# Stores issued from GpSimd's queue, loads alone on SyncE's, in a one-core decoder layer

## The chip, the cores and the metric

The kernel is one program on 1 core of a Trainium2 chip. The metric is the device time of one execution in microseconds (us); the median of several runs counts. The core's engines work from separate instruction streams: TensorE (PE, with its weight loads as PEld), VectorE (DVE), ScalarE (ACT), GpSimd (POOL) and SyncE (SP). SP computes nothing here; it issues the DMAs, and its stream is named SPq in the profile. An engine's stream runs in order: an instruction that waits for a semaphore holds up all that stands behind it.

## The reference

One layer of a decoder over 1024 tokens of width 1024, all float32. It runs a half-step SwiGLU feed-forward (hidden width 2816), one projection of the normalised rows into all branches' operands, three attentions (with forget bias, sparse over the 256 best keys of an indexer, and into 256 memory tokens), a gated merge, and a second half-step feed-forward:

```python
h = h + 0.5 * swiglu(rmsnorm(h, ffn1_norm[l]), ffn1_w_gate[l], ffn1_w_up[l], ffn1_w_down[l])
u = rmsnorm(h, mix_norm[l])
(fq, fk, fv, ff, dq, dk, dv, iq, ik, iw, mq, g) = jnp.split(u @ w_in[l], SPLIT_POINTS, axis=-1)
...
o_a = fox_attention(fq, fk, fv, logf)
o_b = dsa_attention(dq, dk, dv, iq, ik, iw, k_sel)
o_c = memory_attention(mq, km, vm)
...
proj = jnp.einsum('bsnw,nwd->bsnd', branches, w_branch[l])
gates = jax.nn.sigmoid(g.reshape(B, S, N_BRANCHES, D))
h = h + jnp.sum(gates * proj, axis=2) @ w_out[l]
h = h + 0.5 * swiglu(rmsnorm(h, ffn2_norm[l]), ffn2_w_gate[l], ffn2_w_up[l], ffn2_w_down[l])
```

## The kernel before

Every matrix product is made of three products of numbers split into a high and a low part, so each weight tile that arrives (`wS`) is cast by ACT (`wH`) and the rest is taken by DVE (`wL`, line 230's `split`). Two slots of `wS`, or four while a second pool is open, hold arriving weights; the next load into a slot can go out when DVE has finished with it.

The stages follow one another on PE:

- Memory keys and values and the first normalisation (0 to about 70 us in the trace), then feed-forward 1 to about 708 us. Its hidden rows go to a scratch tensor in HBM (`hid_s`, 44 stores of 512 KB out of `gu` tiles, which have three buffers) and come back for the second half.
- The projection, about 715 to 1138 us. It is made in blocks of 512 columns: `mq` (memory queries), `iq` (indexer queries), `fk`, `fq`, `fv` (forgetting attention), `dq` (sparse queries). A block takes its 128-row units one by one: 24 matmuls into `tm`, then a norm on ACT and DVE, a transpose on PE and a split into `th` and `tl` (`turn`, line 801). Each half is stored to the block's scratch tensor as 128 partitions of 4 runs of 128 numbers (128x4x128, runs of 512 bytes). `th` and `tl` have two buffers each, so unit n+2 may write its `th` only when the store of unit n's has landed. `fox_values` (line 1533) splits values into an `iqs` tile of 128x8x128, with two buffers too. Units of the indexer load their stored queries back (`iqs<-iq_s`, line 1472) and score keys (`isc`).
- The heads, about 1138 to 1550 us: queries, keys, values and masks are loaded back; outputs go to `o_s` and the sums' reciprocals to `r_s`. The gate projection fills gaps on PE from 715 us on (`gate`, 48 stores of `sg`, two buffers, to `g_s`).
- The merge to about 1803 us (`branch`, line 1183): gates come back as `bg` (three buffers), partial sums go to `mg_s` and come back as `bm`; the tile `bg` is what is stored to `mg_s`.
- The output projection and norm to about 1915 us, with 8 stores of `h` to `h_s`; then feed-forward 2, whose last step adds into `rows` and stores 8 row tiles to `out`.

The order in which the work is written comes from a planner (`_Flow`) with costs of PE, ACT and DVE; it knows nothing of queues. A scheduler of the language then lists the instructions of every engine, with a model of each DMA's duration in which the queue counts, so a change of queue can swap neighbours on all engines.

All DMAs go through two helpers, `load` (line 172) and `store` (line 175). In the kernel before both use SP's queue, so SP's stream holds 326 stores between its loads. POOL's stream holds the constants at the start and 32 small memsets for the rotary tables (line 844). The program is built with this line, 1705, which sets aside room for the descriptors of DMAs that GpSimd issues:

```python
nc = bacc.Bacc("TRN2", target_bir_lowering=False, num_devices=1, dynamic_dma_scratch_size=1024)
```

Of the kernel before, what the change touches and what calls it, by code (L numbers as in the profile page):

```python
# [155 lines left out]
def trunk_layer_kernel(  # L156
# [5 lines left out]
    nc = tc.nc  # L162
# [6 lines left out]
    def plain(ap):  # L169
        return ap.bitcast(F32) if ap.dtype == F32R else ap  # L170
# [2 lines left out]
        nc.sync.dma_start(plain(o), plain(i))  # L173

    def store(o, i):
        nc.sync.dma_start(plain(o), plain(i))

    class Pool:

# [50 lines left out]
    def split(high, low, v):  # L230
        A.copy(high, v)
        V.tensor_sub(low, v, high.bitcast(F32))
# [194 lines left out]
    class FeedForward:  # L427
# [57 lines left out]
        def job(self, j):  # L485
# [41 lines left out]
            if not gate:  # L527
                for i in range(2):
                    store(hid_s[j // 2 + i * HF], u[:, 2 * i:2 * i + 2].rearrange("p a t -> p (a t)"))
# [233 lines left out]
    def scratch(name, shape):  # L763
        return dram.tile(shape, F32, name=name)
# [8 lines left out]
    fv_s = scratch("fv_s", [8, P, NT, P])  # L773
# [41 lines left out]
    def store_pairs(dst, t, parts):  # L815
        for i, th in enumerate(parts):
            store(dst[i].rearrange("(a b) d t -> (b d) a t", b=2)[:, :, t * P:(t + 1) * P], th)


    def mem_keys(tp):  # L820
        def consume(t, pt):
            xn = head_norm(tp, pt, 4, 2)
            yield
            for i, v in enumerate(turn(tp, xn)):
                store(km_s[:, :, i].rearrange("h p m -> p h m")[:, :, t * P:(t + 1) * P], v)
        return consume
# [706 lines left out]
    def fox_values(t, pt):  # L1533
        vt = tp.tile([P, 8, P], F32R, tag="iqs", name="iqs", bufs=2)
        split(vt[:, :, 0:64], vt[:, :, 64:128], pt.rearrange("p (h d) -> p h d", h=8))
        store(fv_s.rearrange("h p t d -> p h t d")[:, :, t], vt)
        return
        yield

    blocks = [(mq_block, normed(mq_s, 4, gmx[:, 0:1])), (mk_block(C_IQ), index_queries),  # L1540
              (mk_block(C_FK), normed(fk_s, 8, None)), (mk_block(C_FQ), normed(fq_s, 8, gfx[:, 0:1])),
              (mk_block(C_FV), fox_values), (mk_block(C_DQ), sparse_queries)]
    chains = block_chains(blocks, uh, ul, NT)
    fl.run(chains[:2] + [prep] + chains[2:], width=5, filler=gates_f, background=sel_c, margin=0.5)
# [100 lines left out]
    h = [h2[:, t] for t in range(NT)]  # L1645
# [70 lines left out]
```

## Time and profile before

| | us |
|---|---|
| median of 3 runs (2552.12 to 2558.94) | 2553.32 |
| the profiled execution, its own time | 2555.42 |
| span of its trace, first to last instruction | 2553.4 |
| PE busy in the span | 2426.6 (95%) |
| DVE busy | 1641.0 (64%) |
| ACT busy | 1146.6 (45%) |
| POOL busy | 2.2 |

PE's mean granted clock is 0.978 of full speed. One DMA queue carries 349.62 MB in 297744 packets. An engine's idle time costs something only where the chain of waits that ends last runs through it, so the views to read are the busy time by stage, the waits by engine, and the chain. Time outside the span (2555.42 - 2553.4 = 2.0 us) is taken as fixed.

### The profile page before, as it was taken

The numbers are of one execution on the slowest core, as the hardware profiler recorded it, in microseconds if no ns is written. First come the engines' busy times: TensorE is split into PE (matmuls) and PEld (weight loads), VectorE is DVE, ScalarE is ACT, GpSimd is POOL, SyncE is SP. The second block draws the span as 40 slices with busy tenths as digits, with TensorE's granted clock in tenths as the row PEclk, the third lists the DMA queues.
The fourth block names the chain that finished last, engine by engine and source line by source line (L and its number), as shares of the span: only waits on it lengthen the run. The fifth ranks groups of instructions, "written<-read, shape, count | busy, mean of one in ns | idle before, by whom it ended". The sixth has DMA issues, their size and how long they took to land.

```text
span 2553.4 us, 31738 instructions
## 1 busy us (share of the span) xinstructions
PE 2426.6 (95%) x11532; PEld 2007.0 (79%) x11532; DVE 1641.0 (64%) x3405; ACT 1146.6 (45%) x1904; POOL 2.2 (0%) x40
## 2 busy tenths in 40 slices
PE   6999999999999999989999998999979999999998
PEld 4788888888777878767777886877768888888887
DVE  7855555488757578685667556777376554554885
ACT  5533333333433366657886555543144333333332
POOL 0000000000000000000000000000000000000000
PEclk9899999999999999998999999999989999999999
DMA  7222222474334534544455535756422222225743
GB/s 232 75 80 78 91 84 79 158 302 137 127 123 144 158 106 133 157 141 147 122 156 141 146 108 177 235 173 226 169 85 66 91 66 91 91 71 191 271 151 129
DMA packets 297900, 351.64 MB, mean 138 GB/s; under 512 B 18792, under 2 KB 199688, under 8 KB 297744
## 3 DMA queue, kind: packets, MB, share of 16 engines
q1 hardware_dynamic: 297744, 349.62, 42.8%
q8 instruction: 90, 1.47, 0.2%
q14 instruction: 66, 0.54, 0.1%
HBM read 254.98 MB, written 93.54 MB: 136 GB/s over the span
## 4 chain that ended last, share of the span: by engine, by line
PE 72%; DVE 12%; ACT 7%; DMA 5%; issue 4%; SPq 0%; ACTq 0%; DVEq 0%
PE gx L51 19%; PE gy L51 14%; PE tm L51 8%; PE dx L51 8%; PE dy L51 7%; PE gate L51 6%; ACT junk L51 3%; PE br L51 3%; DVE wL L51 2%; PE po L51 2%; PE pT L51 2%; PE sp L51 2%; DMA wS<-in_w_in 1%; DMA bg<-g_s 1%; ACT ns L51 1%
## 5 line engine op out<-in xcount | busy, mean ns | idle before, releaser
L51 ACT CAST wH<-wS 128x1024 fp32r<-128x1024 f32 x238 | 225.5, 953 | 303.1 <-PE gy L51 102.8
L51 PE MATMUL gx<-th,wH 128*128 128x512 f32 x880 | 318.3, 394 | 7.2 <-ACT th L51 7.2
L51 DVE TENSOR_TENSOR wL<-wS,wH 128x1024 fp32r<-128x1024 f32 x238 | 260.3, 1099 | 88.4 <-ACT wH L51 87.7
L51 PE MATMUL gx<-th,wL 128*128 128x512 f32 x704 | 275.5, 391 | 0.0
L51 PE MATMUL tm<-wH,uh 128*128 128x512 f32 x496 | 200.5, 405 | 9.2 <-ACT wH L51 5.6
L51 PE MATMUL gy<-th,wH 128*128 128x512 f32 x528 | 206.3, 391 | 1.2 <-ACT th L51 1.2
L51 PE MATMUL gx<-tl,wH 128*128 128x512 f32 x528 | 205.4, 389 | 0.0
L51 PE MATMUL gy<-th,wL 128*128 128x512 f32 x528 | 205.4, 389 | 0.0
L51 PE MATMUL gy<-tl,wH 128*128 128x512 f32 x528 | 205.4, 389 | 0.0
L51 ACT ACTIVATE junk<-wk,sn 128x384 bf16<-128x384 f32 (+5 forms) x186 | 164.3, 883 | 89.4 <-DVE sn L51 77.2
L51 PEld LDWEIGHTS gx<-th,wH 128*128 128x128 f32 x880 | 167.5, 191 | 43.1 <-ACT th L51 8.0
L51 PE MATMUL tm<-wL,uh 128*128 128x512 f32 x496 | 197.0, 397 | 1.8 <-DVE wL L51 1.0
L51 PE MATMUL tm<-wH,ul 128*128 128x512 f32 x496 | 196.6, 396 | 0.0
L51 ACT CAST wH<-S 128x1024 fp32r<-128x1024 f32 x88 | 92.3, 1051 | 170.3 <-PE gy L51 167.0
L51 DVE TENSOR_TENSOR wL<-S,wH 128x1024 fp32r<-128x1024 f32 x88 | 107.5, 1223 | 87.8 <-ACT wH L51 87.8
L51 DVE TENSOR_TENSOR gu<-gu,gy 128x512 f32<-128x512 f32 x88 | 60.3, 685 | 157.3 <-PE gy L51 81.6
L51 PE MATMUL gate<-uh,wH 128*128 128x512 f32 x384 | 157.5, 410 | 0.0
L51 DVE TENSOR_TENSOR pl<-pT,ph 128x512 fp32r<-128x512 f32 (+1 forms) x176 | 109.8, 637 | 73.6 <-ACT ph L51 72.9
L51 PEld LDWEIGHTS gx<-th,wL 128*128 128x128 f32 x704 | 133.3, 189 | 27.8
L51 PE MATMUL gate<-uh,wL 128*128 128x512 f32 x384 | 153.4, 400 | 0.0
L51 PE MATMUL gate<-ul,wH 128*128 128x512 f32 x384 | 153.0, 398 | 0.0
L51 PE MATMUL dx<-wH 128*128 128x512 f32 x352 | 137.5, 391 | 2.2 <-DVE rows L51 2.1
(265 smaller groups left out, 5196.9 us busy)
## 6 DMA issues: line engine op xcount, KB each, us to landing
wS<-in_ffn_w_down SPq DMA_DIRECT2D x70, 512.0 KB
wS<-in_w_in SPq DMA_DIRECT2D x48, 512.0 KB
wS<-in_ffn_w_gate SPq DMA_DIRECT2D x44, 512.0 KB
wS<-in_ffn_w_up SPq DMA_DIRECT2D x44, 512.0 KB
hid_s<-gu SPq DMA_DIRECT2D x44, 512.0 KB
a<-hid_s SPq DMA_DIRECT2D x30, 512.0 KB
g_s<-sg SPq DMA_DIRECT2D x48, 256.0 KB
bg<-g_s SPq DMA_DIRECT2D x48, 256.0 KB
```

Source lines behind the costliest of these rows:

```text
L51: return fn(*a, **k)
```

## The change

`store` issues on GpSimd's queue, `load` stays on SP's. With that, POOL's stream holds all stores, in an order of its own, and SP's holds loads alone. `fox_values` stores its tile in two halves of four heads, so 8 stores become 16 and there are 334 in all.

```diff
     def store(o, i):
-        nc.sync.dma_start(plain(o), plain(i))
+        nc.gpsimd.dma_start(plain(o), plain(i))
...
     def fox_values(t, pt):
         vt = tp.tile([P, 8, P], F32R, tag="iqs", name="iqs", bufs=2)
         split(vt[:, :, 0:64], vt[:, :, 64:128], pt.rearrange("p (h d) -> p h d", h=8))
-        store(fv_s.rearrange("h p t d -> p h t d")[:, :, t], vt)
+        for i in (0, 4):
+            store(fv_s[i:i + 4].rearrange("h p t d -> p h t d")[:, :, t], vt[:, i:i + 4])
```

The order of PE's matmuls stays the same but for small swaps (the gate products stand between the same units of the projection). The DMAs' order is shown at three places. First, SP's stream before, at the end of the `fq` block and the start of `fv` in the projection (`wk` is a load of indexer scores, `mk` the mask made from them):

```order
L176 DMA fq_s<-tl 128x4x128
L173 DMA wS<-in_w_in 128x2x512 x2
L176 DMA fq_s<-th 128x4x128
L176 DMA fq_s<-tl 128x4x128
L173 DMA wS<-in_w_in 128x2x512 x2
L176 DMA fv_s<-iqs 128x8x128
L176 DMA fq_s<-th 128x4x128
L176 DMA fv_s<-iqs 128x8x128
L176 DMA fq_s<-tl 128x4x128
L173 DMA wk<-sc_s 128x896
L176 DMA fv_s<-iqs 128x8x128
L176 DMA mask_s<-mk 128x512
```

Now POOL's stream after the change, at the same place:

```order
L176 DMA sc_s<-acc 128x1024
L176 DMA fq_s<-th 128x4x128
L176 DMA fq_s<-tl 128x4x128
L176 DMA fq_s<-th 128x4x128
L176 DMA fq_s<-tl 128x4x128
L176 DMA fv_s<-iqs 128x4x128 x2
L176 DMA fq_s<-th 128x4x128
L176 DMA fv_s<-iqs 128x4x128 x2
L176 DMA fq_s<-tl 128x4x128
L176 DMA mask_s<-mk 128x512
L176 DMA fv_s<-iqs 128x4x128 x12
L176 DMA dq_s<-th 128x4x128
```

The weight loads no longer stand between the stores, and the fv stores have become sixteen of the size of the others. From the first `fq` store to the last `fv` store POOL's stream holds 32 of these, one `sc_s` and one `mask_s`.

Second, SP's stream before at the end of `dq`, where the loads of the first memory head follow:

```order
L176 DMA dq_s<-tl 128x4x128
L176 DMA g_s<-sg 128x512
L176 DMA dq_s<-th 128x4x128
L176 DMA dq_s<-tl 128x4x128
L173 DMA wS<-in_w_in 128x8x128
L173 DMA qs<-mq_s 128x1024
L173 DMA vs<-mq_s 128x1024
L173 DMA km<-km_s 128x512
```

And SP's stream after, at those loads:

```order
L173 DMA wS<-in_w_in 128x8x128 x3
L173 DMA wk<-sc_s 128x1024
L173 DMA wS<-in_w_in 128x8x128
L173 DMA qs<-mq_s 128x1024
L173 DMA vs<-mq_s 128x1024
L173 DMA km<-km_s 128x512
```

The loads of queries and keys have kept the weight load ahead of them and lost the stores.

Third, SP's stream before in the merge, where a row of reciprocal sums (`rs`) is stored and read back (`oR`):

```order
L173 DMA bm<-mg_s 128x512
L176 DMA o_s<-os 64x512
L173 DMA bg<-g_s 128x512
L176 DMA r_s<-rs 8x128
L176 DMA mg_s<-bg 128x512
```

And POOL's stream after, towards the end of the merge:

```order
L176 DMA mg_s<-bg 128x512 x3
L176 DMA o_s<-os 64x512
L176 DMA r_s<-rs 8x128
L176 DMA mg_s<-bg 128x512
```

The store of `rs` stands behind other stores only; the load into `bg` ahead of it is gone from its stream.

## Rows read from the trace of the kernel before

**Rows 1.** The page's part 1: busy time and share of the span.
```profile
PE 2426.6 (95%) x11532; PEld 2007.0 (79%) x11532; DVE 1641.0 (64%) x3405; ACT 1146.6 (45%) x1904; POOL 2.2 (0%) x40
```

**Rows 2.** Windows: stretch, its us; busy us by engine; PE clock, DMA share, GB/s.
```profile
128.00:700.00 572.00, 570.26 (x2517) 471.47 (x2516) 349.65 (x438) 206.12 (x263) 0.00 (x0) 1.00 0.38 127
...
777.00:1138.00 361.00, 347.08 (x1581) 281.96 (x1581) 269.63 (x933) 189.44 (x373) 0.00 (x0) 0.98 0.46 132
...
1550.00:1803.00 253.00, 229.35 (x1219) 191.68 (x1218) 189.97 (x367) 114.00 (x214) 0.00 (x0) 0.97 0.67 216
...
1920.00:2490.00 570.00, 569.89 (x2514) 471.66 (x2513) 342.34 (x402) 205.96 (x262) 0.00 (x0) 1.00 0.36 122
```

**Rows 3.** Waits of SP's queue: waiter <- releaser: us in total, times, longest.
```profile
SPq L173 <- DVE wL L51: 715.9, 156, 32.4
SPq L176 <- DVE gu L51: 219.2, 44, 9.6
SPq L176 <- ACT th L51: 177.1, 39, 14.1
```

**Rows 4.** Waits of ACT and PE for loads.
```profile
ACT wH L51 <- DMA wS<-in_w_in: 23.1, 15, 4.5
...
PE spm L51 <- DMA km<-km_s: 6.8, 2, 4.6
```

**Rows 5.** Tile views of five scratch tensors: stores; issue ns min/median/max, first to last start.
```profile
L176 SPq DMA_DIRECT2D mq_s<-th x8: 359/360/367, 777.4 to 823.2; - x8
...
L176 SPq DMA_DIRECT2D fk_s<-th x8: 359/360/385, 905.4 to 968.9; - x8
...
L176 SPq DMA_DIRECT2D fq_s<-th x8: 359/360/422, 978.6 to 1034.6; - x8
...
L176 SPq DMA_DIRECT2D fv_s<-iqs x8: 359/360/499, 1029.4 to 1071.9; - x8
...
L176 SPq DMA_DIRECT2D dq_s<-th x8: 359/360/370, 1093.5 to 1136.5; - x8
```

**Rows 6.** Timeline of SP in the iq block: start us, us, engine, line, op, out<-in.
```profile
849.18 0.37 SPq L176 DMA_DIRECT2D iq_s<-th  x1
850.78 0.36 SPq L176 DMA_DIRECT2D iq_s<-tl  x1
851.36 2.19 SPq L173 DMA_DIRECT2D iqs<-iq_s  x2
```

**Rows 7.** The chain that ended last, in the merge: start us, us, what.
```profile
1702.58 3.42 DMA mg_s<-bg
...
1710.19 2.90 DMA r_s<-rs
```

**Rows 8.** Timeline of SP at the end of the dq block.
```profile
1137.33 0.36 SPq L176 DMA_DIRECT2D dq_s<-tl  x1
1137.74 0.55 SPq L173 DMA_DIRECT2D wS<-in_w_in  x1
```

**Rows 9.** Timeline of DVE at three places; in brackets idle time before, and releaser.
```profile
1135.48 1.23 DVE L51 TENSOR_TENSOR wL<-wS,wH 128x1024 fp32r<-128x1024 f32 x1
...
1706.82 0.27 DVE L51 COPY rs<-rT 8x128 f32<-8x128 f32 x1
...
1866.44 1.28 DVE L51 SCALAR_TENSOR_TENSOR h<-h,rs_y,gain_row 128x1024 f32<-128x1024 f32 x1 [1.62 <-DMA h_s<-h]
```

**Rows 10.** Timeline of DVE at the end.
```profile
2545.36 2.73 DVE L51 SCALAR_TENSOR_TENSOR rows<-dx,rows 128x512 f32<-128x512 f32 x4 [4.40 <-PE dx L51]
```

**Rows 11.** Timeline of SP at the end.
```profile
2546.08 2.81 SPq L176 DMA_DIRECT2D out<-rows  x4
```

**Rows 12.** The page's part 5: busy us, mean ns of one | idle before, releaser.
```profile
L51 DVE TENSOR_TENSOR wL<-wS,wH 128x1024 fp32r<-128x1024 f32 x238 | 260.3, 1099 | 88.4 <-ACT wH L51 87.7
```

**Rows 13.** Tile view of inv_freq: the rotary memsets and their reader.
```profile
L844 POOL MEMSET inv_freq<- x32: 98/98/100, 744.7 to 745.7; 128x1 f32 x32
L51 DVE TENSOR_TENSOR angles<-pos_f,inv_freq x1: 426/426/426, 754.9 to 754.9; 128x256 f32<-128x256 f32 x1
```

## The prediction

> **What bounds the kernel now.** I read the page's busy times first. PE is busy 95% of the span [rows 1], so at most 126.8 us (2553.4 - 2426.6) can be won, and any stall of PE is paid in full. Next the windows by stage [rows 2]: both feed-forwards run with PE busy throughout (570.26 of 572 us, 569.89 of 570). PE's idle time that DMAs could touch lies in the projection (361.0 - 347.1 = 13.9 us) and the merge (23.7 us). Then the waits [rows 3]: the longest in total on SP's queue are of loads for DVE to free a weight slot (715.9 us), after that come stores that wait for what they store (219.2 us for `gu`, 177.1 for `th`). While SP stands in one of the latter, the loads behind it stand too. That is what the change takes away. What it could pay is seen on the other side [rows 4]: ACT waited 23.1 us for weights of the projection, PE itself 6.8 us for `km`.
>
> **What is moved.** All 334 stores go to POOL, which has 2.2 us of work [rows 1]. No trace here shows a store on POOL, so its service is bounded from the nearest rows. Two prices matter: how soon POOL can issue the next one, and how long one takes to land.
>
> Landing, as it is: the store of `iq_s<-th` is issued at 849.18 and the load that reads it goes out at 851.36 [rows 6], so a 256 KB store of 128x4x128 lands in at most 2.2 us from SP. From POOL I bound it by 2.2 and by twice that, 4.4 (making the descriptors in software costs as much as the whole trip), and take 3.4: the chain has the trip of a 256 KB store beside other traffic at 3.42 us [rows 7], and the projection has traffic beside its stores at a DMA share of 0.46 [rows 2].
>
> Issue: SP takes 0.36 us for one [rows 5]. For POOL the ends are 0.36 (no dearer) and 3.4 (nothing overlaps). For stores with long rows I take 1.0, the middle of the two as a ratio. For the 128x4x128 stores I take the upper end: one must have landed before the next is issued. The reason is in the kernel: it sets aside 1024 bytes for such descriptors, and the edit halves the `fv` store, whose size is double theirs; if double does not fit, two of them at once hardly do.
>
> [...]
>
> **The bursts of the projection.** The stall arises through the buffers: unit n+2 writes `th` on ACT only when unit n's store has landed. Behind ACT's waiting split stand the next unit's square, the relu of index scores and the weight casts, and PE waits for all of them. So before a block's last unit, all its stores but the last four must have gone (for `fv` the last four halves). With 3.4 us a piece:
> - `mq`: 12 stores need 40.8 us; the units' first stores span 823.2 - 777.4 = 45.8, less 0.8 for the split ahead of the store: 45.0. No stall.
> - `fk`: 12 and 4 others at 1.0 need 44.8, in 63.5. None. The `iq` block has six units in about the time of eight; none.
> - `fq` and `fv` together: 16 + 12 = 28 and 2 others need 97.2 us; 978.6 to 1071.9, less 1.3 for both splits, gives 92.0. Stall 5.2.
> - `dq`: 12 and 2 others need 42.8, in 1136.5 - 1093.5 - 0.8 = 42.2. Stall 0.6.
>
> Together +5.8 us [rows 5].
>
> **Landings that are waited for.** Each is 3.4 - 2.2 = 1.2 us later. On the chain I count six: two of `mg_s` (3.42 us and one like it) and one of `r_s` (2.90) in the merge [rows 7], the `iq_s` reload at the first score [rows 6], the `h_s` store that DVE awaited for 1.62 us before it normalises in place [rows 9], and the last `out` store. 6 x 1.2 = +7.2.
>
> **The end.** DVE finishes four row tiles from 2545.36 on in 2.73 us [rows 10], the first at about 2546.05. SP issues them by 2546.08 + 2.81 = 2548.9 [rows 11]. POOL needs 4 x 1.0 from 2546.1: 2550.1. +1.2.
>
> **What is won.** Where a load stood behind a store without another reason. At 1137.33 SP issues the last `dq` store and at 1137.74 the weight load ahead of the memory heads' queries [rows 8]; DVE had freed a slot at 1135.48 + 1.23 = 1136.71 [rows 9]. So 1.0 of the 6.8 us before `km`. In the merge `rs` is ready at 1707.09 [rows 9] and its store is issued at 1710.19 [rows 7], behind a load into `bg`: 3.1 us. Together -4.1.
>
> **What costs nothing.** The 44 `hid_s` stores: PE is full there and `gu` has three buffers, so a job's store has longer than a job (570 us for 22 pairs, 26 us a pair) to land; the cover goes only if a store takes some 20 us. The 48 `g_s` stores: two `sg` buffers, and one is filled every 9 us (412 us of heads for fewer than 48). The rotary memsets now stand behind two `g_s` stores; they ended at 745.7 and are read at 754.9 [rows 13], so they can be 9 us late.
>
> **The sum.** 5.8 + 7.2 + 1.2 - 4.1 = +10.1 on the profiled execution's 2555.4 (2.1 above the median of 2553.3): 2565.5, which is 2563 as a median.
>
> **Rivals.**
> [...]
> - No difference: a store takes 2.9 or less. Then 28 x 2.9 + 2 = 83.2 fits in 92.0 and no burst stalls; 6 x 0.7 + 1.2 - 4.1 = +1.3, 2555. For it: 2.2 from SP, and the likely surcharge is unknown.
> - Faster: landing again 2.9 or less, and free loads pay more than the two places I found. All 6.8 us before `km`, a third of ACT's 23.1 (7.7, the rest being idle time off the path) and the 3.1 of `rs` go: 5.4 - 17.6 = -12.2, 2541. It decides where weight loads went out late because of a store by 4.5 us or more, the longest such wait. Against: 156 loads waited for DVE's slot, which stays.
>
> **How the numbers follow.** My forecast has 0.40, its own range 2556 (3.1 us a store: no burst, 5.4 + 1.2 - 4.1) to 2577 (3.7: 13.6 + 4.2 in bursts, 9.0 + 1.2 - 4.1). The slow rival has 0.20, no difference 0.27, faster 0.13. Within 0.3% is 2545.7 to 2561.0, about what a measurement here can tell from no change. Same: 0.27 and 0.04 of the forecast's lower part, 0.31. Faster: 0.13, and 0.01 of the second rival's edge. Slower: 0.55. The range for eight in ten goes from 2546, leaving out most of the fast rival, to 2620, leaving out the slow rival's upper half.
>
> **What would show it.** Right: POOL issuing 128x4x128 stores no closer than about 3.4 us while it has a backlog; ACT's `th` and `iqs` splits waiting for stores in `fv` and `dq`, by some 6 us; feed-forwards unchanged in length; `rs` stored within a microsecond. Wrong: these stores issued a microsecond apart (two at once do fit), or spaced 4.5 us and more; the projection as long as before or tens of us longer; waits of ACT for weights gone.

## The result and the profile after

The changed kernel takes 2580.06 us (median of 4 runs, 2573.85 to 2582.76), the one before beside it 2552.79. The ratio is 1.0098, 95% interval 1.0074 to 1.0122: slower by 25 us, between 19 and 31. The profiled execution took 2573.85 us, the shortest of the four; its span is 2572.1, which is 18.7 more than before.

First the rows that answer to [rows 1] and [rows 2]. Part 1 of the page of after:

```profile
PE 2429.3 (94%) x11532; PEld 2009.4 (78%) x11532; DVE 1645.8 (64%) x3405; ACT 1145.7 (45%) x1904; POOL 204.8 (8%) x374
```

PE does the same work, and POOL now has 204.8 us of it for 334 stores. The windows of after (columns as in [rows 2]). The second and the third are the projection from its first `mq` store on and the merge; they start and end at the same matmuls as those of [rows 2]. The first and the last lie in the feed-forwards:

```profile
128.00:700.00 572.00, 570.77 (x2520) 472.01 (x2519) 351.31 (x438) 205.45 (x263) 12.80 (x24) 1.00 0.38 127
779.60:1160.80 381.20, 351.78 (x1581) 283.79 (x1580) 272.90 (x945) 194.28 (x382) 83.20 (x119) 0.96 0.36 123
1568.50:1824.80 256.30, 233.57 (x1220) 195.47 (x1218) 190.28 (x367) 113.77 (x214) 29.06 (x54) 0.95 0.65 209
1940.00:2510.00 570.00, 569.90 (x2515) 471.88 (x2514) 343.98 (x403) 205.04 (x262) 13.87 (x26) 1.00 0.37 123
```

The feed-forwards are as full as before. The projection's stretch is 20.2 us longer (381.2, 361.0 before) with the same 1581 matmuls in it. PE is idle there for 381.2 - 351.8 = 29.4 us, where it was 13.9; the other 4.7 us are the matmuls themselves, at a mean granted clock of 0.96 where it was 0.98. The merge is 3.3 us longer, none of it idle time of PE.

What SP waits for in after, beside [rows 3]:

```profile
SPq L173 <- DVE wL L51: 1099.7, 164, 30.1
SPq L173 <- DMA mg_s<-bg: 86.0, 27, 6.1
```

No store stands ahead of a load on SP's stream any more. Its loads wait longer instead: for DVE's weight slots (1099.7 us, 715.9 before), as one expects when SP comes to the same wait sooner, and for stores to `mg_s` to land (86.0 us, 33.7 before). The waits for loads that [rows 4] shows, in after:

```profile
ACT wH L51 <- DMA wS<-in_w_in: 26.5, 13, 6.8
...
PE spm L51 <- DMA km<-km_s: 8.6, 2, 6.4
```

Both have grown. So at these two places the freed loads paid nothing.

Where the time went is read by taking the same matmul (by its tile names and count) in two traces, and subtracting its start in before. This is worked out from the traces, in us:

| matmul at, in before | after | room 1408 | + old order | + h_s on SP |
|---|---|---|---|---|
| 690, feed-forward 1 | -1.1 | -3.2 | +0.4 | -3.3 |
| 734, start of the projection | +2.9 | +0.5 | +5.3 | -3.4 |
| 815, end of mq | +2.8 | +0.6 | +4.9 | -5.0 |
| 868, iq block | +7.4 | +0.9 | +4.7 | -3.2 |
| 954, fk block | +11.1 | +4.4 | +5.7 | -1.4 |
| 1040, fv block | +16.6 | +10.8 | +7.0 | +0.3 |
| 1120, dq block | +21.9 | +11.5 | +6.4 | -0.2 |
| 1300, heads | +18.8 | +9.3 | +7.3 | -0.3 |
| 1600, merge | +18.8 | +9.2 | +11.2 | -1.8 |
| 1640, merge | +24.5 | +15.8 | +11.9 | -0.1 |
| 1940, feed-forward 2 | +18.2 | +9.0 | +1.3 | -9.6 |

The last three columns are experiments below. A single trace is good for a step of several us at one place and not for a total: the runs of before alone lie between 2543 and 2559, and the last column ends at -9.6 though the median of its kernel equals before's. What all four win between 1640 and 1940 can't be told from chance by it.

### The profile page after: what moved, and what is told of

Same layout as the page of the kernel before. It is cut to its first block, busy times and chain, and to the rows that moved or that the text cites. A ratio compares the mean times of both kernels' runs of the same rounds, so it can differ in the third digit from the quotient of the medians.

```text
span 2572.1 us, 31970 instructions
## 1 busy us (share of the span) xinstructions
PE 2429.3 (94%) x11532; PEld 2009.4 (78%) x11532; DVE 1645.8 (64%) x3405; ACT 1145.7 (45%) x1904; POOL 204.8 (8%) x374
## 3 DMA queue, kind: packets, MB, share of 16 engines
q0 software_dynamic: 28640, 94.61, 10.0%
## 4 chain that ended last, share of the span: by engine, by line
PE 59%; issue 16%; DVE 12%; ACT 6%; DMA 5%; POOL 2%; SPq 0%; POOLq 0%; ACTq 0%; DVEq 0%
PE gx L51 19%; PE gy L51 14%; PE dy L51 6%; PE dx L51 6%; PE tm L51 6%; PE gate L51 3%; ACT junk L51 3%; DVE wL L51 2%; DMA wS<-in_w_in 1%; PE nar L51 1%; PE br L51 1%; ACT wH L51 1%; DVE rs_a L51 1%; DVE hsq L51 1%; ACT ns L51 1%
## 5 line engine op out<-in xcount | busy, mean ns | idle before, releaser
L51 DVE TENSOR_TENSOR S<-wS 128x512 f32<-128x512 f32 x88 | 57.3, 688 | 160.8 <-DMA wS<-in_ffn_w_gate 92.6
```

Source lines behind the costliest of these rows:

```text
L51: return fn(*a, **k)
```

## The experiments

The theories: A, the room for GpSimd's descriptors makes the 128x4x128 stores follow one another; B, a store costs more on a second queue whatever its size, since transfers compete and land later; C, GpSimd's own work on a store or DVE's work spaces the stores; and, added after the first runs, D, the scheduler's new order of the instructions costs time by itself. The first runs have `sp_store` beside `store`, which issues on SP as before; `store` issues on GpSimd.

**The blocks' stores back on SP.**

```diff
-            store(dst[i].rearrange("(a b) d t -> (b d) a t", b=2)[:, :, t * P:(t + 1) * P], th)
+            sp_store(dst[i].rearrange("(a b) d t -> (b d) a t", b=2)[:, :, t * P:(t + 1) * P], th)
...
-        for i in (0, 4):
-            store(fv_s[i:i + 4].rearrange("h p t d -> p h t d")[:, :, t], vt[:, i:i + 4])
+        sp_store(fv_s.rearrange("h p t d -> p h t d")[:, :, t], vt)
```

> The 128x4x128 stores of the projection (mq, iq, fk, fq, dq; fv unsplit) go back to SyncE; all other stores stay on GpSimd. Theory A (the room for GpSimd's descriptors holds one such store, and they are spaced 2.85 us and more, which holds up th, tl and iqs): the projection, 20 us longer in the trace after, is within 4 us of before; the start of the projection (+4), the merge (+4) and the heads (-5) stay as after; about 2556 to 2560. Theory B (any store on GpSimd's queue costs, since transfers on two queues compete and land later): the projection keeps 10 us or more, 2568 or more.

Measured: 2563.45 us, ratio 1.0037 (1.0023 to 1.0051). Some 16 us come back (1.0098 - 1.0037), so these stores carry the larger part; but 10 us stay, more than theory A allowed, and 6 of them arise between 976 and 1006 us, where this kernel has none of them on GpSimd's queue. Neither theory had that. In the traces TensorE, ScalarE and VectorE run their instructions, and SP its loads, in the same order here as in after, so the 16 us are a comparison with the order held, and the 6 us are for theory D to explain.

**Only the blocks' stores on GpSimd** (all other calls read `sp_store`).

> The reverse: only the 128x4x128 stores (fv in two halves) are issued by GpSimd, all other stores by SyncE. Theory A: the projection is 15 to 22 us longer than before and nothing else moves, 2568 to 2576. Theory B: under 8 us, 2555 to 2561.

Measured: 2564.21 us, ratio 1.0043 (1.0028 to 1.0058): 11 us, between the two forecasts. The block stores cost something without the others: `iq_s`, `fv_s` and `dq_s` stores stand in its chain. But its order of instructions is a third one, neither that of before nor that of after, so not all of the 11 us need be theirs; and the two halves (10 and 11) do not quite make the 25 to 27 of the whole.

**More room.**

```diff
-    nc = bacc.Bacc("TRN2", target_bir_lowering=False, num_devices=1, dynamic_dma_scratch_size=1024)
+    nc = bacc.Bacc("TRN2", target_bir_lowering=False, num_devices=1, dynamic_dma_scratch_size=1408)
```

> After, with dynamic_dma_scratch_size=1408 instead of 1024, nothing else. [...]

Measured: 2564.60 us, ratio 1.0044 (1.0030 to 1.0058): within the 2560 to 2570 that theory A had for two stores at a time, and below the 2575 to 2583 of theory C. The order of all instructions in its trace is that of after, so some 14 us (1.0098 - 1.0044) belong to the room alone. The timeline of POOL in after, in the fv block (columns as in [rows 9]):

```profile
1070.16 0.76 POOL L176 DMA_DIRECT2D fv_s<-iqs  x1 [1.55 <-issue]
1073.04 0.75 POOL L176 DMA_DIRECT2D fv_s<-iqs  x1 [2.12 <-issue]
1075.89 0.76 POOL L176 DMA_DIRECT2D fv_s<-iqs  x1 [2.10 <-issue]
```

and the same block with 1408:

```profile
1054.44 1.50 POOL L176 DMA_DIRECT2D fv_s<-iqs  x2 [2.01 <-DVE iqs L51]
1060.84 1.50 POOL L176 DMA_DIRECT2D fv_s<-iqs  x2 [4.90 <-DVE iqs L51]
```

In after a piece follows 2.85 us behind the last; with more room two go in 1.50 us, and POOL waits for DVE's split, which is the data. The chain of after tells what the 2.85 are:

```profile
1073.04 2.55 DMA fv_s<-iqs
```

This store lands at 1075.59, and the next starts at 1075.89, 0.30 us later. In the trace of after 79 stores of this size directly follow another one on POOL's stream. None starts earlier than 0.30 us behind the landing of the one ahead, and 69 start within 0.4 us of it; with 1408, 49 of the 79 start before the one ahead has landed. Theory C falls.

**The smallest room that should do.** The same edit with 1088.

> [...] If stores are admitted whole when their descriptors fit, this is as good as 1408: 2561 to 2568, spacing 0.75 us within a pair. If the room's effect grows with its size, hardly better than 1024: 2573 to 2582.

Measured: 2566.64 us, ratio 1.0053 (1.0040 to 1.0067), the stores again in pairs of 1.50 us. 64 bytes more give back 11 us; 320 more on top add little that can be told apart (the intervals overlap). With 1024 bytes, 94% of 1088, none of the 79 stores starts before the one ahead has landed, so in these runs a store is admitted whole or not at all.

**Only the stores to g_s, o_s and r_s on GpSimd.** The other calls read `sp_store`.

> Only the stores to g_s, o_s and r_s are issued by GpSimd; all others, the projection's among them, by SyncE. If the 5 us that the heads gained after (at 1238 to 1260 us of before) came from loads of queries and keys that stood behind such stores on SyncE's queue, this kernel has them without the loss: 2545 to 2550. If they were a part of earlier delays that was made up, nothing: 2552 to 2556.

Measured: 2559.44 us, ratio 1.0026 (1.0016 to 1.0036). A miss: the win at the first heads is in its trace (+5.5 at 1230 us, 0.0 at 1300), but 5 us are lost at the end of the fk block, where no wait for one of its stores stands. There its list of matmuls differs from before: the indexer's products stand in other places between the block's. The win does not come from the queue alone either: with the order of before and all stores on GpSimd (below) the shift at this place changes by +0.4 us, where it changes by -4.8 in after.

**Parts of that set.** First o_s and r_s alone, then g_s alone.

> Only the stores to o_s and r_s are issued by GpSimd, those to g_s by SyncE again. The earlier run with g_s, o_s and r_s on GpSimd lost 5 us at the end of the fk block, where its list of PE instructions had changed, and won 5 at the first heads of the second attention. If the loss belongs to g_s alone and the win to o_s and r_s, this kernel has the win: 2546 to 2551. If the win needs g_s off SyncE's queue as well, 2552 to 2556.

> Only the stores to g_s are issued by GpSimd. They are far from the path, so by their own cost nothing changes; but the scheduler's list of the indexer's and the block's matmuls around 960 to 1000 us differs from before. If it is this new order that costs the 5 us at the end of the fk block: 2556 to 2561, with the loss at that place and stores of g_s that nobody waits for. If it is not, 2551 to 2556.

Measured: 2560.81 us, ratio 1.0030 (1.0019 to 1.0042), a miss; and 2556.85 us, ratio 1.0016 (1.0004 to 1.0028). The interval of the latter reaches into both forecasts; its trace shows the loss at the place that was named (+1.1 us at 940, +5.3 at 1000). Every subset was slower than before, and not all at the same places. This is what led to theory D.

**h_s back on SP, room 1408.** The eight stores after feed-forward 1 read `sp_store`.

> After with dynamic_dma_scratch_size=1408 (2564.6 us by itself) and the eight stores of h_s after feed-forward 1 on SyncE again, where the first weight loads of the projection stand ahead of them. If the 4 us at the start of the projection come from these stores, which on GpSimd's queue overtake the weight loads: 2558 to 2562 and a first load that lands in 3.5 to 4.5 us instead of 7.3. If something else delays that load, 2563 to 2567.

Measured: 2562.59 us, ratio 1.0039 (1.0024 to 1.0055). The place is mended: the first weight load lands in 3.61 us, and in its trace the start of the projection is at -0.3 where feed-forward 1 was at -0.6. In the time 2 us less than 1408 alone can't be told from none, so this run settles the place and not the price.

**The old order, stores on GpSimd, room 1408.** To part queue and order, the order of before is written into the kernel as a list (`_ORDER`, ranks of the instructions by engine), and each is chained to the one ahead of it by an edge that means order only:

```diff
+        for d in step:
+            at += d
+            i = mine[at]
+            before = last.get(str(i.engine))
+            if before is not None:
+                tc.add_manual_dep(i, before.name, mybir.DependencyInfo(
+                    mybir.DependencyClass.NoSync, mybir.DependencyReason.DATA), reason="pinned")
+            last[str(i.engine)] = i
...
         trunk_layer_kernel(tc, *args)
+        pinned(tc, nc)
```

> All 326 stores on GpSimd with dynamic_dma_scratch_size=1408 (fv stored whole), but every engine's instructions, the loads on SyncE and the stores on GpSimd stand in the order of the kernel before, held by edges that say order and no wait. Only the queue of the stores differs from before. If the 11 us that stay with two stores in the room come from the order that the scheduler made for the new queue (theory D): 2553 to 2559, with the 4 us at the start of the projection and little else. If they are the price of the second queue itself, transfers that land later (theory B): 2560 to 2567.

Measured: 2557.15 us, ratio 1.0020 (1.0008 to 1.0032). In its trace TensorE and ScalarE have before's order throughout and VectorE but for one small instruction that stands four places later; SP's loads and POOL's stores have their order within before's SP stream. Against 1408 alone that is 6 us (1.0044 - 1.0020); fv goes whole here, which is the one other difference.

**The new order, stores on SP.** The same device with the order of after for the three engines, and the kernel before otherwise.

> The reverse: all stores on SyncE and fv stored whole, as before, but the instructions of TensorE, ScalarE and VectorE stand in the order that they have after; SyncE's own order is the scheduler's. Theory D: the new order costs by itself, 2558 to 2565, at the end of the fk block and in the merge. Theory B: it costs nothing without the second queue, 2551 to 2556.

Measured: 2567.76 us, ratio 1.0056 (1.0043 to 1.0068): slower by 14 us without one store on GpSimd, more than forecast. It loses at the places that 1408 loses (fk block, and 8 us in the merge, between 1610 and 1620 us of before). SP's own list is another one here than in before or after, so the 14 us need not be the price that the same order has in after. Theory D holds, theory B does not account for these 6 us.

**The old order, h_s on SP.** As two runs above, with `sp_store` for the eight stores of h_s.

> As the run with all stores on GpSimd, two in the room and the order of before (2557.2 us), but the eight stores of h_s after feed-forward 1 stay on SyncE, behind the first weight loads of the projection. If the 4 us left are those at the start of the projection: 2551 to 2555, no difference from before. If they are spread over later landings: 2556 to 2559.

Measured: 2551.66 us beside 2551.26, ratio 1.0007 (0.9997 to 1.0017): no difference from before. So 318 of 326 stores are on GpSimd and, costs and gains together, cost nothing that these runs can show, which is the end of theory B as a general rule.

The rows of the chain at the start of the projection, the first weight load: before, after, and this run.

```profile
709.37 3.52 DMA wS<-in_w_in
```

```profile
708.31 7.29 DMA wS<-in_w_in
```

```profile
706.12 3.24 DMA wS<-in_w_in
```

In before SP issued one h_s store, six weight loads, and then three more stores. On a queue of their own four h_s stores of 512 KB go out at 706.15 to 708.55, beside the first weight load, which lands in 7.29 us instead of 3.52, and PE stands. The trace shows the load taking twice the time with 2 MB of stores beside it; how they hold it up is not shown.

**r_s alone, old order.** The kernel before with one queue changed, for 20 small stores.

> The kernel before with one thing changed: the 20 stores to r_s go to GpSimd's queue, in the order of before on all engines. In the merge a store of r_s stood 3.1 us behind a load into bg; with the order kept and all stores on GpSimd that place gave back 4.7 us. If this is won by r_s alone: 2547 to 2550. If SyncE's stores of mg_s make the reload as late as before: 2551 to 2555.

Measured: 2552.74 us beside 2551.26, ratio 1.0004 (0.9993 to 1.0014). The place is 2.9 us better in its trace (+0.6 at 1700 us, -2.3 at 1720); in the time no gain can be told. No kernel of this study is faster than before.

## Why the prediction was right, and where not

It said slower, and gave 2563 in a range of 2546 to 2620; 2580 is in the range, above the forecast's own upper end of 2577 and well below the slow rival's 2623. The move is +25 to +27 where +10 was worked out. So the direction was right and its first reason was right, but that 2580 lies within the range is partly luck: the part above 2577 was there for a rival that the runs do not bear out, and most of the added time comes from the room's larger price and from two steps that the sum did not have. By the ratios the 25 us are 14 for the room, 6 for the order, 3 for the `h_s` stores and 2 for all the rest. (In the chances one hundredth is counted twice; it changes nothing.) By its steps:

- **One store at a time: right, and shown.** With 1024 bytes the room holds one 128x4x128 store, with 1088 and with 1408 two. The reason given was the halved `fv` store; no run issues a whole one with 1024 bytes, so what was inferred from it is shown and the reason is not.
- **The price of a store: too high when alone, too low in traffic.** 3.4 us were taken. Measured are about 2.85 (2.55 to land and 0.30 more) for most and 4.2 beside loads, as from 861.27 to 865.50 in the iq block; over the backlog from the first `fq` store to the last of `fv` it is 3.25 on the mean (31 steps in 100.9 us, one `sc_s` and one `mask_s` among them). With little beside it a store lands in 2.5 to 2.6 us, as 62 of the 92 block stores do. The upper bound of 4.4 was the author's assumption: POOL is busy 0.75 us with a store, and no run shows what part of the 2.55 us to land is the making of descriptors.
- **The bursts: the right mechanism, too small and not in all its places.** Forecast 5.8 us, 5.2 at fv and 0.6 at dq. After against 1408, same order, loses 5.7 us in the fv block (PE at 1087 to 1097 us of after, 4.0 of it one wait of ACT, below) and nothing in dq. The size at fv is partly luck: with the measured 3.25, which has the two other stores in it, the prediction's own sum of 28 stores fills 91.0 of its 92.0 us and gives no stall. It asked only whether all but four stores are gone before the last unit, and the waits came at the fourth and fifth of eight. (In the trace of after eight `fq` stores, not four as in the list shown before, stand between the last `sc_s` and the first fv store.) After also loses 4 us from the end of `mq` through the iq block, 3 of them at two reloads of queries; the iq block was put down as no stall. There it is not buffers: the reload needs both halves, and they now go one behind the other. By the times the room costs some 14 us; the trace of after is its fastest run and shows 9.

The wait of ACT in the fv block of after, which 1408 has not:

```profile
ACT iqs L51 <- DMA fv_s<-iqs: 5.2, 2, 4.0
```

And the iq block in the chain of after, against [rows 6]:

```profile
853.84 0.77 POOL iq_s L176
...
856.80 4.17 DMA iq_s<-tl
860.98 3.81 DMA iqs<-iq_s
```

In before both reloads had been issued by 853.55 (851.36 + 2.19), 4.4 us behind the first store; now the second goes out at 860.98, 7.1 us behind it.

- **Landings, +7.2: too large, as far as the rows show.** It charged 1.2 us at six places for a landing from GpSimd that is longer than one from SP. A lone 256 KB store lands in 2.5 us from GpSimd, 2.2 at most from SP [rows 6]. Of the six places, the longest wait for `h_s` is 1.41 us in after, where it was 1.62 (though all such waits together are 3.2 us, 2.1 before); the `r_s` store of the merge takes 2.60 with the old order, where it took 2.90; from the last `out` store to the end it is 0.8 more (next point). For the others no run has a clean comparison. The times alone do not refute the term: with order and h_s as before, landings, end and gains together are 1.8 us, interval -0.8 to 4.3, and the prediction's three terms make 7.2 + 1.2 - 4.1 = 4.3.
- **The end, +1.2: the number as forecast, the reason not.** The trace has +17.5 at the last matmuls and 18.7 in the span. But POOL issues the last four stores 0.68 us apart and not 1.0, as SP did; that is the rate at which DVE finishes the tiles. The 1.2 are 0.4 before the first of them, and 0.8 from the last issue to the end of the span (6.07 us, where SP's took 5.24). The latter is the landing that was charged among the six as well.
- **Gains, -4.1: one came and one did not.** The store of `rs` no longer waits (row below). The wait before `km` grew from 6.8 us to 8.6. In the run with `r_s` alone on GpSimd no gain can be told in the time.
- **Left out: the order, 6 us.** The prediction took the swaps on DVE, ACT and PE for nothing. In the traces another instruction than before stands in 427 of 11532 places on TensorE, 414 of 1900 on ScalarE and 1107 of 3405 on VectorE. Two places can be followed over all the runs. At the end of the fk block (940 to 1000 us of before) the eight traces with after's list on these three engines lose 3.8 to 6.1 us, whichever queue the blocks' stores use, and the four with before's list 1.5 at most. In the merge (1600 to 1640 us) six traces with after's list lose 4.0 to 7.5 us and five with before's 0.6 to 1.8. One place shows why a swap costs. In the merge of after the reload of `o_s` stands behind a load into `bg` that waits for a store to land. SP's timeline and the DVE row that waits:

```profile
1617.37 0.32 SPq L173 DMA_DIRECT2D bg<-g_s  x1
1617.78 3.03 SPq L173 DMA_DIRECT2D qs<-dq_s  x4
1620.90 0.54 SPq L173 DMA_DIRECT2D oR<-r_s  x1
1626.99 0.33 SPq L173 DMA_DIRECT2D bg<-g_s  x1
1627.42 0.37 SPq L173 DMA_DIRECT2D wS<-o_s  x1
```

```profile
1631.81 1.23 DVE L51 TENSOR_TENSOR wS<-wS,oR 128x1024 f32<-128x1024 f32 x1 [4.25 <-DMA wS<-o_s]
```

The chain between them has the store that the `bg` load waited for:

```profile
1620.91 5.94 DMA mg_s<-bg
```

Four loads of `qs` go out in one piece ahead of it (before they stood between stores), the store takes 5.94 us, and DVE with all behind it waits 4.25 us. With the old order one trace, with all stores on GpSimd, still loses 4.5 us shortly before, at 1595 to 1600 us; the one with `h_s` on SP does not.

- **Left out: stores that overtake loads, about 4 us at their place.** It looked for loads that stores hold up, and not for loads that had been let go first. At the start of the projection the traces of after, 1408, 1088, the old order and the run with the blocks on SP lose 3.9 to 4.6 us, the two with `h_s` back on SP 0.3 at most. In the time it is 3 us (1.0020 to 1.0007) with overlapping intervals, so the place is shown and the price is not.

The slow rival of the chances, 0.20, had 1.1 us more for each store, a wait for one instruction of DVE. No run shows that term. In its place the issue of a block's store takes 750 to 772 ns in all 92, in a stretch where DVE is busy 272.9 of 381.2 us; here the 16 pieces of fv (ns, min/median/max):

```profile
L176 POOL DMA_DIRECT2D fv_s<-iqs x16: 750/756/762, 1050.6 to 1104.3; - x16
```

The rows of `rs` in the run with the old order, ready at 1718.04 and stored at 1718.33, against the 3.1 us from ready to issue in before:

```profile
1717.77 0.27 DVE L51 COPY rs<-rT 8x128 f32<-8x128 f32 x1
```

```profile
1718.33 2.60 DMA r_s<-rs
1720.94 3.80 DMA oR<-r_s
```

Its place gains 4.7 us there (+11.0 before it, +6.3 after).

What stays open: how the 14 us of the room divide between the iq block and fv in a median run, since only the fastest was profiled; which swaps of the order cost what and why; and what the `h_s` stores cost in a median run.

## What to carry to other kernels

Where stores have moved to GpSimd's queue, see in the trace whether those of the most runs start only when the one ahead has landed; here 64 bytes more of room gave back 11 us. The bytes of a store did not tell it: in after four `h_s` stores of 512 KB in 128 rows went out within 2.40 us, each with 3.0 us or more to land, while 256 KB in 512 runs went one at a time. One queue also kept an order here: the first weight load, which SP had issued ahead of three of the stores, landed in 3.52 us and not 7.29. A second queue gives that up, so leave on the loads' queue the stores that fall together with the first loads of a stage. Where a scheduler lists the instructions, compare any change of queue with the order held fixed, or one measures the new order.

## What was not expected of the hardware

- In after a 128x4x128 store behind another one starts 0.30 us after that one's landing at the earliest, in 69 of 79 cases within 0.4 us of it. The profile blames whatever ended last ("issue", "DVE sn", "ACT junk") for that wait; only the landing times in the chain show it.
- POOL is busy 0.53 us for a store of 128 rows, 0.75 for one of 512 runs, 0.90 for one of 1024 (the whole fv stores of the run with the old order): eight times the runs take 1.7 times as long.
- The same 94.6 MB of stores are 28640 packets on GpSimd's queue, while SP's has 80864 fewer than before, and the engines' share of time is 41.6% in sum, where it was 42.8%. The queues of after:

```profile
q1 hardware_dynamic: 216880, 255.02, 31.6%
q0 software_dynamic: 28640, 94.61, 10.0%
```
